# RWKV head pairs: all TensorE work in an order held by the source, with projections fed in stated numbers between the products

## The chip, the cores and the metric

The kernel runs on one core of a Trainium2 chip. The metric is the device time of one execution in microseconds (us). The kernel before takes 2841.09 us, the median of 3 runs (2839.93 to 2842.29). One more execution was taken by the hardware profiler; it took 2842.14 us, and its span, from the first to the last instruction that the profile shows, is 2839.8 us.

Five engines work side by side, each through its own queue of instructions: TensorE (PE: matrix products and transposes; PEld is its weight load), VectorE (DVE), ScalarE (ACT), GpSimd (POOL) and SyncE (SP, which here only issues transfers). They wait for each other by semaphores.

## The reference

One layer of a hybrid decoder block for x of 512 tokens by 2048 channels, in float32. One large input product gives the channels of both mixers and of two gates; the RWKV-7 mixer and a sliding-window attention run in parallel, are merged by sigmoid gates and projected out, and a gated convolutional FFN follows. The part that the change touches is the RWKV mixer with 16 heads of 64 channels:

```python
def rwkv7_mix(zs, w0, w2, a0, a2, g2, k_k, k_a, r_k, gn_w, gn_b):
    ...
    r, k, v, wd, ad, gd = jnp.split(zs, [o1, o2, o3, o4, o5], axis=-1)
    w = -jax.nn.softplus(-(w0 + jnp.tanh(wd) @ w2)) - 0.5
    decay = jnp.exp(-jnp.exp(w.astype(f32)))
    a = jax.nn.sigmoid(a0 + ad @ a2)
    g = jax.nn.sigmoid(gd) @ g2
    kk = (k * k_k).reshape(hd).astype(f32)
    kk = kk / jnp.maximum(jnp.sqrt(jnp.sum(kk * kk, axis=-1, keepdims=True)), 1e-12)
    k = k * (1.0 + (a - 1.0) * k_a)
    ...
    def step(state, inp):
        r_t, k_t, v_t, w_t, ka_t, kb_t = inp
        sa = jnp.einsum('bhvk,bhk->bhv', state, ka_t)
        state = (state * w_t[:, :, None, :] + sa[..., None] * kb_t[:, :, None, :]
                 + v_t[..., None] * k_t[:, :, None, :])
        y = jnp.einsum('bhvk,bhk->bhv', state, r_t)
        return state, y
    ...
    y = ((y - mu) * lax.rsqrt(var + GN_EPS)).reshape(B, S, RW_DIM)
    y = y * gn_w.astype(f32) + gn_b.astype(f32)
    bonus = jnp.sum(rh * kh * r_k.astype(f32), axis=-1, keepdims=True) * vh
    out = (y + bonus.reshape(B, S, RW_DIM)) * g.astype(f32)
    return out.astype(zs.dtype)
```

zs is the input product with a token shift: each channel is mixed with the token before by a factor mu of its own.

## The kernel before

The program goes through its stages in this order: norm and attention (up to about 310 us), the RWKV head pairs (332 to 1109 us), the gates that are left and the branch products (from 1109 us), the output product, and the FFN up and down.

**A projection.** Every 128 columns of the input product are a tile `acc` (128 x 512) in PSUM. It takes 48 products of TensorE: for each of 16 blocks of 128 input channels three products, since operands are split into a high and a low part (`whi`, `wlo`, `xhi`, `xlo`; L255, L256, L257). The weights come in pieces of four blocks: SP loads `raw` (L235), ScalarE rounds the high part `whi` (L238), VectorE subtracts for `wlo` (L239). Four pairs of `whi` and `wlo` are held, so 4 x 12 = 48 products can be ready ahead. In this document "projections" are these single products.

**A head pair.** The 16 heads are worked through in 8 pairs, and the recurrence in 8 chunks of 64 tokens (NCH = 8, C = 64). `early(p)` makes a pair's operands: the tiles k, r and v with the token shift (ScalarE writes `zpad`, L536, and VectorE combines, L537: `kz`, `rz`, `vz`), the norm of kk (sums of squares on TensorE, L369; eleven small steps of an inverse root on VectorE, L183 to L192; then `head_rows`, which turns the result, `rsT`, and sends it through DRAM, `rsd`, to be read back spread over the partitions, `rsb`), the decay (a lora product, tanh, a running sum `Ei` by two scans, L659, two exponentials), and `BKK`, `BAR`, the keys and queries of all chunks. `late(p)` does the pair's products: "grams" of the keys with the queries (L719, masked by VectorE into `OW` and `AM`, L722), the values transposed and centred (`VV`, L752), the decayed keys (`BKK` times `ee`, L742) transposed (L758) and copied by ScalarE (`KD`, `KO`, L762 and L763), the products for all chunks (`KV`, `GV`, L625), and then a triangular inverse built in levels m = 2, 4, 8, 16, 32. A level has a product with `AI` and one with `BT` (both L773 and L774, 16 small products each); VectorE works in between (reduce L776, mask L790, cast L791, subtract L792, into `XIW`), and behind it a transposition (L802) whose result VectorE and ScalarE copy into `BT` (L806, L808). Then comes a chain over the 8 chunks of 22 links, each a small product of TensorE that waits for VectorE or ScalarE: `psG`, `psU`, `psS`, with `G`, `UU` and the state `SS`. `final(p)` does the outputs (46 small products), the group norm (`yd`), four transposes (L855), and the gate from a lora product (L620).

**What sets the order.** Instructions of an engine run in the order in which the program holds them. A scheduler makes that order when the program is built, from the source order and its own estimates of durations; only what is wrapped in `pin` keeps the source's order. Before the change, pinned were the grams, the pair's products over all chunks (L625) and the chain's `psU`. The loop calls `late(p)`, then `early(p+1)`, `final(p)` and three gate projections (`emit_gate`), and the scheduler mixes the projections of the next pair between the products of this one. PSUM holds three `acc`, three `bulk` and two `chn` tiles.

## Time and profile before

| | us |
|---|---|
| median of 3 runs | 2841.09 |
| profiled execution | 2842.14 |
| its span | 2839.8 |
| TensorE busy in the span | 2772.6 (98%) |
| VectorE busy | 1975.7 (70%) |
| ScalarE busy | 1289.0 (45%) |
| a steady head pair (first gram to first gram, 630.51 to 729.29) | 98.78 |
| the last pair (1026.08 to the last output product, 1108.78) | 82.70 |

Times are counted from the span's start. A row of the timeline gives the start, the duration, the engine and line, the operation with what it writes and reads, and in brackets how long the engine had been idle and what ended that. A large product's duration (0.39 us) is longer than the distance to the next one's start (0.227 us), because products overlap in the array; so distances of starts are used to measure a gap. A row of the waits names the engine and line that waited, what ended the wait, the sum in us, the number of times and the longest.

### The profile page before, as it was taken

How to read it: one execution, taken by the hardware profiler on the slowest of the kernel's cores; microseconds unless marked ns; L12 is line 12 of the kernel's file. 1: busy time of each engine (PE TensorE's matmuls, PEld its weight loads, DVE VectorE, ACT ScalarE, POOL GpSimd, SP SyncE). 2: the span in 40 equal slices, each digit the busy share in tenths (PEclk: the TensorE clock that was granted, in tenths of full speed). 3: DMA queues.
4: the chain of work that ended last, by engine and by line, in shares of the span. 5: the costliest groups of instructions: out<-in, count | busy, mean ns of one | idle time of the engine just before them, and what ended most of it. 6: DMA issues, size and time to landing. Idle time of an engine off the chain costs nothing.

```text
span 2839.8 us, 48133 instructions
## 1 busy us (share of the span) xinstructions
PE 2772.6 (98%) x18722; PEld 2413.2 (85%) x18722; DVE 1975.7 (70%) x3312; ACT 1289.0 (45%) x2075; POOL 230.8 (8%) x307
## 2 busy tenths in 40 slices
PE   7999999999999999999999999999999999999999
PEld 6888777777777777788888999999999999788887
DVE  5566677778777774455668777777777778655555
ACT  5345344334433433322465555555555555444444
POOL 0101000000000001011000101010101110000000
PEclk9999999999999999999999999999999999999999
DMA  6865676676667668888777789888988897877775
GB/s 190 232 155 152 174 181 166 159 179 162 164 152 177 164 173 240 241 245 275 245 260 200 220 237 245 225 226 232 244 229 224 231 241 227 313 242 241 257 257 189
DMA packets 223860, 608.06 MB, mean 214 GB/s; under 512 B 24576, under 2 KB 44688, under 8 KB 222608
## 3 DMA queue, kind: packets, MB, share of 16 engines
q1 hardware_dynamic: 156096, 432.49, 47.4%
q0 software_dynamic: 36832, 134.24, 24.6%
q10 hardware_dynamic: 30704, 38.27, 3.9%
q8 instruction: 146, 2.39, 0.3%
q14 instruction: 82, 0.67, 0.1%
HBM read 554.23 MB, written 174.40 MB: 257 GB/s over the span
## 4 chain that ended last, share of the span: by engine, by line
PE 86%; DVE 8%; DMA 2%; issue 1%; ACT 1%; ACTq 0%; SPq 0%; DVEq 0%
PE X L1164 18%; PE X L1031 11%; PE acc L255 9%; PE acc L257 9%; PE acc L256 9%; PE Y L1031 9%; PE Y L1164 8%; PE Z L1164 4%; PE bulk L625 1%; PE bulk L773 1%; DMA raw<-in_w_z_dram 1%; PE mi L508 1%; DMA raw<-in_w_dn_dram 1%; DVE BT L741 1%; PE bulk L802 1%
## 5 line engine op out<-in xcount | busy, mean ns | idle before, releaser
L257 PE MATMUL acc<-xhi,wlo 128*128 128x512 f32 x1120 | 450.3, 402 | 6.8 <-DVE wlo L239 6.8
L255 PE MATMUL acc<-xhi,whi 128*128 128x512 f32 x1120 | 450.1, 402 | 2.4 <-ACT whi L238 2.4
L256 PE MATMUL acc<-xlo,whi 128*128 128x512 f32 x1120 | 449.1, 401 | 0.0
L238 ACT ACTIVATE whi<-raw 128x512 fp32r<-128x512 f32 x352 | 220.7, 630 | 466.7 <-PE acc L256 353.3
L1024 DVE TENSOR_TENSOR wlo<-raw,whi 128x1024 fp32r<-128x1024 f32 x210 | 257.1, 1225 | 205.9 <-ACT whi L1023 204.3
L239 DVE TENSOR_TENSOR wlo<-raw,whi 128x512 fp32r<-128x512 f32 x352 | 240.3, 688 | 183.2 <-ACT whi L238 177.3
L1023 ACT ACTIVATE whi<-raw 128x1024 fp32r<-128x1024 f32 x210 | 222.6, 1060 | 291.0 <-PE X L1031 154.2
L1164 PE MATMUL X<-b,whi 128*128 128x256 f32 x1472 | 269.2, 283 | 2.3 <-DVE u L1184 0.9
L1147 DVE TENSOR_TENSOR wlo<-raw,whi 128x1024 fp32r<-128x1024 f32 x176 | 215.1, 1223 | 76.8 <-ACT whi L1146 76.5
L1164 PE MATMUL X<-t,whi 128*128 128x256 f32 x1408 | 259.1, 284 | 8.8 <-DVE u L1184 8.3
L1164 PE MATMUL Y<-t,whi 128*128 128x256 f32 x1408 | 257.1, 283 | 0.0
L257 PEld LDWEIGHTS acc<-xhi,wlo 128*128 128x128 f32 x1120 | 211.6, 189 | 46.4 <-DVE wlo L239 10.7
L255 PEld LDWEIGHTS acc<-xhi,whi 128*128 128x128 f32 x1120 | 211.4, 189 | 40.2 <-ACT whi L238 2.8
L256 PEld LDWEIGHTS acc<-xlo,whi 128*128 128x128 f32 x1120 | 211.8, 189 | 36.0
L1146 ACT ACTIVATE whi<-a 128x1024 fp32r<-128x1024 f32 x132 | 139.4, 1056 | 214.7 <-DVE a L1140 213.3
L1164 PEld LDWEIGHTS X<-b,whi 128*128 128x128 f32 x1472 | 229.5, 192 | 3.1 <-issue 2.4
L1164 PEld LDWEIGHTS X<-t,whi 128*128 128x128 f32 x1408 | 221.0, 193 | 9.3 <-DVE u L1184 5.7
L1164 PEld LDWEIGHTS Y<-t,whi 128*128 128x128 f32 x1408 | 219.6, 192 | 0.0
L1164 PE MATMUL X<-b,wlo 128*128 128x256 f32 x736 | 208.4, 283 | 2.1 <-DVE wlo L1147 2.1
L1147 DVE TENSOR_TENSOR wlo<-a,whi 128x1024 fp32r<-128x1024 f32 x132 | 161.7, 1226 | 67.4 <-ACT whi L1146 66.7
L1164 PE MATMUL X<-t,wlo 128*128 128x256 f32 x704 | 200.1, 284 | 0.0
L1164 PE MATMUL Y<-t,wlo 128*128 128x256 f32 x704 | 199.2, 283 | 0.0
(680 smaller groups left out, 5870.3 us busy)
## 6 DMA issues: line engine op xcount, KB each, us to landing
raw<-in_w_up_dram SPq DMA_DIRECT2D x180, 512.0 KB
raw<-in_w_z_dram SPq DMA_DIRECT2D x288, 256.0 KB
s_dn<-in_w_dn_dram POOLq DMA_DIRECT2D x88, 512.0 KB, 6.5
raw<-in_w_up_dram POOLq DMA_DIRECT2D x88, 512.0 KB, 8.3
raw<-s_dn SPq DMA_DIRECT2D x88, 512.0 KB
raw<-in_w_dn_dram SPq DMA_DIRECT2D x66, 512.0 KB
a<-in_w_up_dram SPq DMA_DIRECT2D x48, 512.0 KB
s_dn<-in_w_dn_dram SPq DMA_DIRECT2D x44, 512.0 KB
```

The lines of the kernel that those rows point to most:

```text
L238: pin(act.activation(hi, raw, AF.Copy))
L239: pin(dve.tensor_tensor(lo, raw, hi.bitcast(F32), op=ALU.subtract))
L255: pe.matmul(acc, whi[:, j], xhi[:, k], start=first, stop=False)
L256: pe.matmul(acc, whi[:, j], xlo[:, k], start=False, stop=False)
L257: pe.matmul(acc, wlo[:, j], xhi[:, k], start=False, stop=last)
L508: pe.matmul(ps[:, h], pT[:, kb, h], vt[:, n - 1 + kb, g * HD : (g + 1) * HD], start=kb == kbs[0], stop=kb == kbs[-1])
L1023: act.activation(whi, wr, AF.Copy)
L1024: dve.tensor_tensor(wlo, wr, whi.bitcast(F32), op=ALU.subtract)
L1031: pe.matmul(dst, l[:, q, ts], r[:, es], start=fst and j == 0, stop=lst and j == 2, skip_group_check=True)
L1146: pin(act.activation(hi, t, AF.Copy))
L1147: pin(dve.tensor_tensor(lo, t, hi.bitcast(F32), op=ALU.subtract))
L1164: pin(pe.matmul(ps, l[:, k], r[:, k], start=start and k + i == 0, stop=last and i == 2, skip_group_check=True))
```

## The change

The pair's work is cut into methods of two classes: `Early` (the next pair's operands) and `Pair` (the products). Every product and transpose of TensorE in this stage goes through `mm` or `turn`, which pin it. Projections are made by generators, `tile_job`, one product a step; `feed(n)` issues the next n of them from a list `jobs_bg`, in the order gate, k, r, v, gate, gate for each pair, and six gates in the last pair. The source states the numbers: 38 projections, the first gram, (the previous pair's `back`: transposes of yd), 10, the second gram, 16, the transposes of OW, 18, (the previous pair's `gated`: its lora product), 24, and then in each level the AI product, 14, the BT product, 9, the transposition. Inside the levels stand now: `values` behind BT at m=2, `keys` behind BT at m=4, the next pair's sums of squares at m=8, `inputs` (KV, GV) at m=16, and behind the transposition of m=16 the next pair's `rows` and `decay`; then `rate`, 10, the chain with 3 projections behind each of 22 links, and the outputs. In all 288 projections a pair, 6 tiles. In the level's second half ScalarE's and VectorE's `XIW` now come in the source ahead of `BX`. What VectorE, ScalarE, SP and GpSimd do is still ordered by the scheduler, save that the decay of BKK is issued behind the masks of BT (`issue_after`). The number of instructions is the same on each engine.

How the built order changes is shown at three places, without the rows' numbers.

VectorE at level m=8, before (`half` is what the reduce writes, `rz` the next pair's shifted r; the reduce L776 in the sixth row answers the AI product of the level):

```order
L776 TENSOR_REDUCE half__4848<-bulk 128x8x32
L795 TENSOR_SCALAR BX<-half__4848 64x8x8x4
L798 SCALAR_TENSOR_TENSOR XIW<-half__4848,XIW 128x64x4
L537 SCALAR_TENSOR_TENSOR rz<-acc,omu,zpad_2832 128x512
L806 COPY BT<-bulk 64x8x64
L776 TENSOR_REDUCE half__4884<-bulk 128x8x32
L239 TENSOR_TENSOR wlo<-raw,whi 128x512
L806 COPY BT<-bulk 64x8x64
L790 TENSOR_TENSOR half__4884<-half__4884,cst 128x8x32
L791 CAST XIW<-half__4884 128x8x32
L239 TENSOR_TENSOR wlo<-raw,whi 128x512
L792 TENSOR_TENSOR XIW<-half__4884,XIW 128x8x32
```

and after the change (L855 is the reduce, L893 the copy into BT):

```order
L855 TENSOR_REDUCE half__5030<-bulk 128x8x32
L882 TENSOR_SCALAR BX<-half__5030 64x8x8x4
L239 TENSOR_TENSOR wlo<-raw,whi 128x512
L880 SCALAR_TENSOR_TENSOR XIW<-half__5030,XIW 128x64x4
L893 COPY BT<-bulk 64x8x64
L537 SCALAR_TENSOR_TENSOR rz<-acc,omu,zpad_2832 128x512
L855 TENSOR_REDUCE half__5104<-bulk 128x8x32
L893 COPY BT<-bulk 64x8x64
L871 TENSOR_TENSOR half__5104<-half__5104,cst 128x8x32
L239 TENSOR_TENSOR wlo<-raw,whi 128x512
L872 CAST XIW<-half__5104 128x8x32
L873 TENSOR_TENSOR XIW<-half__5104,XIW 128x8x32
```

The shift of r still stands ahead of the level's reduce, now behind one copy into BT.

ScalarE at the same place, before, where the copies into KD and KO stood ahead of the levels:

```order
L794 ACTIVATE BX<-half__8147 64x8x16x2
L797 ACTIVATE XIW<-half__8147 128x128x2
L808 ACTIVATE BT<-bulk 64x8x64 x2
L238 ACTIVATE whi<-raw 128x512
L794 ACTIVATE BX<-half__8205 64x8x8x4
L797 ACTIVATE XIW<-half__8205 128x64x4
L536 ACTIVATE zpad_2832<-acc,par 128x512
L238 ACTIVATE whi<-raw 128x512
L808 ACTIVATE BT<-bulk 64x8x64 x2
```

and after, where they stand behind the BT product of m=4 (L839 and L840):

```order
L839 ACTIVATE KD<-bulk 64x4x64
L840 ACTIVATE KO<-bulk 64x256
L879 ACTIVATE XIW<-half__8387 128x64x4
L881 ACTIVATE BX<-half__8387 64x8x8x4
L839 ACTIVATE KD<-bulk 64x4x64
L840 ACTIVATE KO<-bulk 64x256
```

Behind these rows come two more pairs of KD and KO, `zpad_2832` and the two copies into BT (L895). So eight copies into KD and KO now stand in front of r's `zpad` and of the copies into BT, with the level's `XIW` and `BX` between them.

VectorE at level m=32 and at the chain's start, after the change. Before, the level's rows from the reduce to the subtraction held only a copy into BT and two `wlo`, and `lw`, the scans, `kk` and what follows stood among the links of the chain:

```order
L855 TENSOR_REDUCE half__5380<-bulk 128x8x32
L893 COPY BT<-bulk 64x8x64
L717 TENSOR_SCALAR lw<-lw 128x512
L871 TENSOR_TENSOR half__5380<-half__5380,cst 128x8x32
L720 SCALAR_TENSOR_TENSOR Ei<-going,lw 128x256 x2
L872 CAST XIW<-half__5380 128x8x32
L239 TENSOR_TENSOR wlo<-raw,whi 128x512
L873 TENSOR_TENSOR XIW<-half__5380,XIW 128x8x32
```

```order
L202 TENSOR_TENSOR wllo<-wl,wlhi 128x256
L731 TENSOR_SCALAR k_5434<-lw,half 128x512
L709 TENSOR_TENSOR kk<-kk,rsb 128x512
L732 TENSOR_TENSOR k_5434<-k_5434,kz 128x512
L733 TENSOR_SCALAR lw<-lw 128x512
L239 TENSOR_TENSOR wlo<-raw,whi 128x512
L735 TENSOR_TENSOR kz<-kk,lw 128x512
L921 TENSOR_TENSOR SS<-KV,link 128x64
```

`lw` and the scans of `Ei` (L717, L720) have moved between the mask (L871, and ahead of it) and the cast (L872), and `kk<-kk,rsb` with three multiplies and a `wlo` ahead of the chain's first `SS`.

The diff, cut to its core ("..." marks what is left out; the methods that are not shown hold the same operations as the functions before):

```diff
+            def mm(*args, **kw):
+                pin(pe.matmul(*args, **kw))
+
+            def turn(*args):
+                pin(pe.transpose(*args))
+
+            jobs_bg = []
+
+            def tile_job(c0, done):
+                acc = accp.tile([P, S], F32, name="acc", tag="acc")
+                src = zt[c0]
+                for k0 in range(0, NK, 4):
+                    whi, wlo = load_w(src[:, k0 : k0 + 4])
+                    for j in range(4):
+                        k = k0 + j
+                        for i, (l, r) in enumerate(((whi, xhi), (whi, xlo), (wlo, xhi))):
+                            mm(acc, l[:, j], r[:, k], start=k + i == 0, stop=k == NK - 1 and i == 2)
+                            if k == NK - 1 and i == 2:
+                                done(acc)
+                            yield
+
+            def gate_job():
+                i = gates.pop(0)
+
+                def done(acc):
+                    g = gp.tile([P, S], F32, name="gt", tag="gt")
+                    act.activation(g, acc, AF.Tanh, scale=0.5)
+                    act.dma_start(gate_d[i * P : (i + 1) * P], g)
+
+                return tile_job(d.c_zr + i * P, done)
+
+            def feed(n):
+                while n and jobs_bg:
+                    if next(jobs_bg[0], True):
+                        jobs_bg.pop(0)
+                    else:
+                        n -= 1
+
...
-            def early(p):
-                wl = lp.tile([P, 2 + NG, P], F32, name="wl", tag="wl", bufs=2)
-                sync.dma_start(wl, a["lora"][p].rearrange("p (k c) -> p k c", c=P))
-                w2a2 = lora_parts(wl, 0)
...
-            def late(p, st):
-                wl, Ei, kk, kb, k2, rz, vz, bon = st
...
-                dve.tensor_tensor(BKK, BKK, ee.unsqueeze(2).to_broadcast([P, NCH, P]), op=ALU.mult)
-                ps = bulk()
-                for t in range(NT):
-                    ts = slice(t * P, (t + 1) * P)
-                    pe.transpose(ps[:, ts], vz[:, ts], ident)
-                vm = wk.tile([P, NCH], F32, name="vm", tag="vm")
...
-            def final(p, st):
-                wl, bon = st
-                ps = bulk()
-                for n in reversed(range(NCH)):
...
-            st = early(0)
...
+            class Early:
+
+                def __init__(self, p):
+                    self.p = p
+                    self.wl = lp.tile([P, 2 + NG, P], F32, name="wl", tag="wl", bufs=2)
+                    sync.dma_start(self.wl, a["lora"][p].rearrange("p (k c) -> p k c", c=P))
+
+                def jobs(self):
+                    p = self.p
+                    return [tile_job(d.c_k + p * P, self.k_in), tile_job(d.c_r + p * P, self.r_in),
+                            tile_job(d.c_v + p * P, self.v_in)]
+
...
+                def rows(self):
+                    rb = head_rows(wk, bulk(), self.rs, "lg", turn=turn)
+                    dve.tensor_tensor(self.kk, self.kk, rb, op=ALU.mult)
+
+                def decay(self):
+                    self.w2a2 = lora_parts(self.wl, 0)
+                    ps = bulk()
+                    lora(ps, self.w2a2, (0,), 0)
...
+            class Pair:
+
+                def __init__(self, st):
...
+                def decayed(self):
+                    with tc.issue_after(self.masked.ins):
+                        dve.tensor_tensor(BKK, BKK, self.st.ee.unsqueeze(2).to_broadcast([P, NCH, P]), op=ALU.mult)
+
+                def keys(self):
+                    self.KO = KO = wk.tile([P, NCH, C], F32, name="KO", tag="ko")
+                    for g in range(2):
+                        ns = slice(g * HN, (g + 1) * HN)
+                        ps = bulk().rearrange("p (n c) -> p n c", c=P)
+                        for j in range(HN):
+                            turn(ps[:, j], BKK[:, g * HN + j], ident)
+                        for lo, hi in HV:
+                            act.activation(KD[lo:hi, ns, lo:hi], ps[0:C, :, lo:hi], AF.Copy)
+                            act.activation(KO[lo:hi, ns], ps[C:P, :, lo:hi], AF.Copy)
+
+                def inputs(self):
...
+                def second(self, m):
+                    xa, IW = self.rows_of(m), self.IW
+                    t = self.by_block(self.mm3(BT, lambda n: IW[:, n].rearrange("p e c -> p (e c)"), lambda n: IW[:, n, 0]), m)
+                    if m != LEVELS[-1]:
+                        act.activation(xa[:, 0], t, AF.Copy, scale=1.0 / SG)
+                        dve.scalar_tensor_tensor(xa[:, 1], t, 1.0 / SG, xa[:, 0], op0=ALU.mult, op1=ALU.subtract)
+                    act.activation(self.altered(BX[0:C, :, 0:C], m), t[0:C], AF.Copy, scale=1.0 / (SG * SG))
+                    dve.tensor_scalar(self.altered(BX[C:P, :, C:P], m), t[C:P], 1.0 / (SG * SG), None, op0=ALU.mult)
...
+            st = Early(0)
+            for job in st.jobs():
+                jobs_bg.append(job)
+            feed(NK * 3)
+            st.stats()
+            feed(NK)
+            st.rows()
+            st.decay()
+            st.rate()
+            feed(NK * 8)
+            st.bonus()
+            st.bonus_sums()
+            gone = None
             for p in range(NP):
-                lt = late(p, st)
-                if p + 1 < NP:
-                    st = early(p + 1)
-                final(p, lt)
-                for _ in range(GATES_PER_PAIR * NK // 16):
-                    emit_gate()
+                last = p == NP - 1
+                nxt = None if last else Early(p + 1)
+                own = [] if last else nxt.jobs()
+                others = [gate_job() for _ in range(min(len(gates), 6 if last else GATES_PER_PAIR))]
+                jobs_bg += others[:1] + own + others[1:]
+                do = Pair(st)
+                st.dense()
+                st.rows_r()
+                if gone:
+                    gone.scaled()
+                feed(38)
+                do.gram(0)
+                if gone:
+                    gone.back()
+                feed(10)
+                do.gram(HN)
+                do.start_x()
+                feed(16)
+                do.start_a()
+                feed(18)
+                do.start_rest()
+                if gone:
+                    gone.gated()
+                feed(24)
+                do.decayed()
+                for m in LEVELS[1:]:
+                    i = LEVELS.index(m)
+                    do.first(m)
+                    feed(14)
+                    do.second(m)
+                    if i == 1:
+                        do.values()
+                    if i == 2:
+                        do.keys()
+                    if nxt and i == 3:
+                        nxt.stats()
+                    if i == 4:
+                        do.inputs()
+                    if m != LEVELS[-1]:
+                        feed(9)
+                        do.turned()
+                    if nxt and i == 4:
+                        nxt.rows()
+                        nxt.decay()
+                if nxt:
+                    nxt.rate()
+                feed(10)
+                for i, _ in enumerate(do.chain()):
+                    feed(3)
+                    if nxt and i == 2:
+                        nxt.bonus()
+                    if nxt and i == 6:
+                        nxt.bonus_sums()
+                do.outputs()
+                gone, st = do, nxt
+            gone.scaled()
+            feed(30)
+            gone.back()
+            feed(12)
+            gone.gated()
+            feed(1000)
 
 
         xbs = ExitStack()
```

384 lines of the change are left out of this document (201 added, 183 removed).

## The prediction

> **What bounds the kernel now.** I read the page first, then the stretches of the RWKV stage one by one, then what TensorE waits for there, then single rows around the waits. From the page:
>
> ```profile
> span 2839.8 us, 48133 instructions
> PE 2772.6 (98%) x18722; PEld 2413.2 (85%) x18722; DVE 1975.7 (70%) x3312; ACT 1289.0 (45%) x2075; POOL 230.8 (8%) x307
> PEclk9999999999999999999999999999999999999999
> ```
>
> TensorE is busy for 98% of the span at the full granted clock. So only its gaps can be won or lost, and a changed order of the same products moves time only through gaps. The next view cuts the span into a steady pair, the last pair, the projections behind it, and a stretch of bare large products. Its columns are the length, the busy time of PE, PEld, DVE, ACT and POOL, the granted clock, the share of the DMA engines, and GB/s:
>
> ```profile
> 630.51:729.29 98.78, 96.05 (x757) 75.06 (x756) 74.60 (x168) 39.53 (x81) 7.09 (x9) 1.00 0.69 167
> 1026.08:1108.78 82.70, 79.95 (x683) 61.77 (x683) 58.65 (x128) 31.85 (x66) 5.68 (x7) 1.00 0.71 178
> 1108.78:1165.00 56.22, 53.86 (x236) 43.96 (x235) 18.52 (x28) 18.62 (x32) 11.47 (x17) 1.00 0.96 299
> ```
> ```profile
> 1260.00:1330.00 70.00, 70.00 (x310) 57.98 (x309) 35.05 (x57) 18.19 (x30) 7.29 (x10) 1.00 0.82 257
> ```
>
> Bare products start every 70.00/310 = 0.226 us (0.227 below). A steady pair holds about 300 of that width (288 projections, 12 lora and similar): 68.1 us. The rest, about 30.7 us, is small products and gaps. The waits that have a name, over all pairs (total, times, longest):
>
> ```profile
> PE bulk L758 <- DVE BKK L742: 7.1, 7, 1.0
> PE acc L257 <- DVE wlo L239: 6.8, 8, 0.8
> PE bulk L855 <- DVE yd L851: 3.6, 8, 0.5
> ...
> PE psG L814 <- DVE SS L828: 0.6, 1, 0.6
> ```
>
> One pair's rows show what they cost, as start to start less 0.227:
>
> ```profile
> 644.72 0.39 PE L256 MATMUL acc<-xlo,whi 128*128 128x512 f32 x1
> 646.13 1.06 PE L758 MATMUL bulk<-ident,BKK 128*128 128x128 f32 x8 [1.01 <-DVE BKK L742]
> ...
> 647.49 0.40 PE L256 MATMUL acc<-xlo,whi 128*128 128x512 f32 x1
> 648.74 0.50 PE L257 MATMUL acc<-xhi,wlo 128*128 128x512 f32 x1 [0.84 <-DVE wlo L239]
> ...
> 674.47 0.47 PE L255 MATMUL acc<-xhi,whi 128*128 128x512 f32 x1
> 674.78 0.39 PE L256 MATMUL acc<-xlo,whi 128*128 128x512 f32 x1
> ...
> 677.30 0.39 PE L255 MATMUL acc<-xhi,whi 128*128 128x512 f32 x1
> 677.81 0.19 PE L773 MATMUL bulk<-XIW,BT 128*128 128x64 f16 x1
> ```
>
> The wait for BKK is 1.18, for wlo 1.02, for yd about 0.6 (0.45 named, plus its entry). Entry into the second product of a level costs 677.81 - 677.30 - 0.227 = 0.28 here, about 1 us over five levels; transposes and grams wait some 0.5 more. Together about **4.1 us of waits in a pair**, 4% of it. The first projection behind a group of small ones takes 0.31 (674.47 to 674.78), 0.08 extra.
>
> **The change part by part.** No instruction is added or removed on any engine. What changes is TensorE's order, and with it, since the order of the vector, scalar and DMA queues is still made by the scheduler around it, what stands in front of what there.
>
> These rows of VectorE stand behind the next steps (start, duration):
>
> ```profile
> 631.05 0.69 DVE L239 TENSOR_TENSOR wlo<-raw,whi 128x512 fp32r<-128x512 f32 x1 [2.02 <-ACT whi L238]
> ...
> 642.79 1.22 DVE L741 TENSOR_TENSOR BT<-AI,cst 64x1024 f16<-64x1024 f16 x1
> ...
> 644.75 1.23 DVE L742 TENSOR_TENSOR BKK<-BKK,ee 128x1024 f32<-128x1024 f32 x1
> ...
> 647.27 0.69 DVE L748 TENSOR_REDUCE vm<-bulk 128x8 f32<-128x512 f32 x1
> 647.99 0.69 DVE L239 TENSOR_TENSOR wlo<-raw,whi 128x512 fp32r<-128x512 f32 x1
> ```
>
> *Removed.* The groups of projections fall from 42 to about 37 in a pair: 5 x 0.08 = -0.4. BKK's transposes move from straight behind the decay multiply into level m=4, over 50 projections (11 us) later: -1.2. yd's transposes now have the first gram and 38 projections ahead of them: -0.6. The wait for wlo came of a vector queue without a weight split from 631.05 to 647.99; now the longest such run is two splits of A and gn (0.69 each, like wlo), two masks and BKK, 3 x 0.69 + 2 x 1.22 + 1.23 = 5.7 us, or 25 projections, and four split buffers hold 48: -1.0.
>
> *Added.* In each level the source now fixes 14 projections between the AI product and the BT product: 0.31 + 13 x 0.227 = 3.26 us. In that time VectorE must reduce, mask, cast and subtract. From 674.47 to 677.81 that chain took 3.34 us with one BT copy and one weight split in it, so 14 projections cover it and nothing else; whatever more stands in front of the subtraction is a wait of TensorE, one for one. The scheduler of before gave 7 to 17. The rows of VectorE, of ScalarE and of SP's queue that price what more stands there:
>
> ```profile
> 592.24 0.17 DVE L192 SCALAR_TENSOR_TENSOR rq<-rq,rq 128x8 f32<-128x8 f32 x1
> 593.05 0.28 DVE L374 COPY rsT<-bulk 8x128 f32<-8x128 f32 x1 [0.65 <-PE bulk L372]
> ...
> 595.77 0.68 DVE L659 TENSOR_TENSOR_SCAN Ei<-going,lw 128x256 f32<-128x256 f32 x1
> ...
> 601.55 0.69 DVE L649 TENSOR_TENSOR kk<-kk,rsb 128x512 f32<-128x512 f32 x1 [0.40 <-DMA rsb<-rsd]
> ...
> 634.91 1.40 DVE L722 TENSOR_TENSOR OW<-bulk,cst 64x512 f32<-64x512 f32 x2 [0.40 <-PE bulk L719]
> ...
> 649.27 1.72 DVE L752 TENSOR_TENSOR VV<-bulk,vm 64x256 f32<-64x256 f32 x4
> ...
> 653.91 0.69 DVE L776 TENSOR_REDUCE half__7006<-bulk 128x256 f32<-128x512 f32 x1
> ...
> 665.85 0.75 DVE L537 SCALAR_TENSOR_TENSOR rz<-acc,omu,zpad 128x512 f32<-128x512 f32 x1 [0.29 <-ACT zpad L536]
> 666.52 0.41 DVE L806 COPY BT<-bulk 64x512 f16<-64x512 f16 x1
> 666.85 0.67 DVE L776 TENSOR_REDUCE half__7122<-bulk 128x256 f32<-128x512 f32 x1
> ```
> ```profile
> 646.79 0.38 ACT L762 ACTIVATE KD<-bulk 64x256 f32<-64x256 f32 x1 [1.01 <-PE bulk L758]
> ...
> 649.93 0.69 ACT L536 ACTIVATE zpad<-acc,par 128x512 f32<-128x512 f32 x1
> ...
> 659.86 1.21 ACT L808 ACTIVATE BT<-bulk 64x512 f16<-64x512 f16 x2 [1.47 <-DVE BT L806]
> ```
> ```profile
> 593.36 0.29 SPq L376 DMA_DIRECT2D rsd<-rsT  x1
> ...
> 597.59 1.12 SPq L380 DMA_DIRECT2D rsb<-rsd  x2
> ```
>
> By level, in the queue order of the changed program:
>
> - m=2. Before, VectorE worked without a pause from the second gram's eviction to the first reduce, 653.91 - 634.91 = 19.0. The values leave this run (VV 1.72, vm 0.85) and one split (0.6); gn and a lora split enter (1.1): 16.9, begun 0.5 after the gram, since the first gram's evictions and the previous pair's gn are just done. TensorE has 58 projections, OW's transposes, six lora products and AI in that time, 15.7, and the reduce could start 0.2 later. It is 1.5 late at most, 0.3 if splits fall out: I take **1.0**.
> - m=4. VV (1.72) and the mean of v (0.85) now stand in front of the BT copy and the reduce. VectorE comes to the copy about 0.8 late: **0.7** (0.2 to 1.1).
> - m=8. ScalarE's queue gets eight KD and KO copies of 0.38 with X and BX between them, then zpad 0.69, then BT 1.21. From the end of the BT product at m=4 (t), ScalarE waits 0.6 for four transposes, so zpad ends at t+5.2. rz on VectorE waits for it, and behind rz stand the reduce and a BT copy. The reduce could start at t+4.1 and starts at t+5.9: **1.4** (0.5 to 1.8).
> - m=16. Eleven small steps of the root (0.17 each) stand between copy, reduce and cast, half of them ahead: **0.4** (0.05 to 0.8).
> - m=32. lw (0.43) and two scans (0.68 each) stand between mask and cast, and lw waits for a tanh behind BT's 1.21: **1.3** (0.3 to 1.8).
> - Chain. kk waits for the norm's round trip through DRAM, 601.55 - 593.05 = 8.5 from rsT, and behind it in VectorE's queue stand kk, k's multiply, lw, a split and kz (4 x 0.69 as kk's row and 0.43 for lw, 3.2) and then the first SS, for which the product of G waits. From rsT TensorE has AI, 14 projections, the wait at m=32, BT, three lora products, ten projections and two links, 10.5: between 0 (DMA early) and 2; **1.2**, nearer to the row. SP's queue carries rsd and rsb as before; raw loads behind rsd wait from 593.36 to 597.59, 4.2 us, under four filled split buffers (48 projections, 10.9 us).
> - Gram and links: **0.3**.
>
> Sum 6.3 us of waits in place of 4.1, less 0.4 of returns: **+1.8 in each of seven pairs, +12.6**. The last pair has no next pair's k, r, v, norm or decay in its queues: 0.3 + 0.7 + 0.3 + 0.3 = 1.6 in place of 4.2, and the returns: **-3.0**.
>
> *Moved.* Three gates go from behind the last pair into pairs, so 168 and not 248 projections cover the loads of the branch stage: 38 us and not 56. The stall there is today:
>
> ```profile
> PE acc L255 <- ACT whi L238: 2.4, 1, 2.4
> ```
>
> It falls about 37 us after the last pair, with DMA at 0.96 in the row above, so loads are behind already. It stays, and up to 4 more may come since the branch weights are wanted 18 us sooner: **+0.5** (-2 to +4). Gate writes and the pair's output write move on ACT's and GpSimd's queues; nobody waits for them before the branch stage.
>
> Sum: 12.6 - 3.0 + 0.5 = +10.1 on the profiled execution's 2842.1 us, which is 1.05 above the median: **2851 us**.
>
> **The rivals.**
>
> *Faster: the fixed counts do cover the queues.* If VectorE and ScalarE reach each reduce on time, the five entries cost 0.28 as at 677.81 and the chain nothing: 1.4 + 0.3 + some 0.2 = 1.9 of waits, -2.2 - 0.4 in a pair, x 7 = -18, -3 for the last: 2841 - 21 = **2820**. For it: BKK, wlo and yd really go, 2.8 in a pair. Against it: at 665.85 rz waited 0.29 for zpad, and the BT copy (666.52) and reduce (666.85) behind it were issued only after it, though the copy's input does not depend on it. A late ScalarE thus delays the reduce. It decides if the lag at an entry is under 0.3.
>
> The Trainium skill, "TensorE: Matmul & The Clock Gate", in the table at its top (row "Engine queue depth"), has ScalarE and VectorE as strict first-in-first-out queues; by that rule this rival needs the queues short, and the trace agrees, with the 0.29 just named.
>
> *Same: the lags are half of mine.* 6.0/2 + 0.3 + 0.9 (entries that remain) = 4.2, returns -0.4: -0.3 x 7 - 3 + 0.5 = -4.6: **2837**. For it: VectorE has 24 us idle in a pair of 98.78 and can catch up.
>
> *Slower still: the norm's round trip or the loads of the tail decide.* If the row comes back 2 us later than 8.5, as in the one pair where G waited 0.6 even with the old order, each of seven pairs pays 1.8 more, or the branch stage pays 4: **2855 to 2868**.
>
> *The clock falls.* If the granted clock went to half for the next 7 projections after each of some 42 new stalls, each stall would lose 7 x 0.227 = 1.6 more: 2851 + 67 = **2918**. Against it: the steady pair with stalls of 1.18 and 1.02 only 2.6 us apart shows a granted clock of 1.00, and so does the stretch with a stall of 2.4.
>
> The Trainium skill, "TensorE: Matmul & The Clock Gate", section "A second HAM failure mode: psum-queue depth-cycling", says that frequent short idles between groups of products can make the clock gate swing to half rate, which is the rule behind this rival; by that rule alone the pair before should have shown it, and the trace does not agree, with its 1.00.
>
> *The change does not do what it says.* TensorE's order is pinned, so it does; but the other queues are not pinned, and my lags rest on their built order.
>
> **How the numbers follow.** A measurement of this kernel can tell 0.2%, 5.7 us, from no change: faster is below 2835.4, slower above 2846.8. My forecast (lags of 5 to 7.5 in a pair) has 0.44, slower still 0.14, the clock 0.02, same 0.22, faster 0.18. A tenth of my forecast's share lies below 2846.8, and a twentieth of the same case below 2835.4, which gives slower 0.56, same 0.25, faster 0.19. The forecast's own range is 2845 to 2859; with the other cases the range is **2827 to 2865**, which leaves out the far half of faster and the end of slower still.
>
> **What would show it.** Right: waits for BKK, yd and wlo are gone from TensorE's list; in their place stand waits of the BT product (XIW, from the subtraction) of 0.5 to 1.5 at m=2, 4, 8 and 32, and one of G for SS; steady pairs of 100 to 101 us, the last of 79 to 80. Wrong: XIW waits below 0.3 each and pairs near 96 would mean that the queues keep up (faster); a G wait over 2 us or a stall over 4 ahead of the branch stage would mean the rival on the slow side; a granted clock below 1.00 in pairs would mean the rival of the clock.

## The result, and the profile after

The changed kernel takes 2882.64 us, the median of 4 runs (2878.38 to 2883.53), against 2841.69 us (2839.93 to 2843.97) of the kernel before: a ratio of 1.0137 with a 95% interval of 1.0123 to 1.0150. It is slower by 1.4%, some 41 us, four times the 10 us that the prediction named. The profiled execution took 2878.38 us (the lowest of its four runs), its span is 2876.6 us, so 36.8 us longer than before's.

The page of the changed kernel, its head and the row of PE, DVE and ACT:

```profile
span 2876.6 us, 48139 instructions
PE 2781.3 (97%) x18722; PEld 2444.3 (85%) x18722; DVE 1972.3 (69%) x3312; ACT 1289.6 (45%) x2075; POOL 229.9 (8%) x307
```

TensorE has the same products as before and is busy for 8.7 us longer in total; the other 28 us are idle time. Busy time is itself a sum of two things, products that ran longer and short delays that went away; they are taken apart below. What TensorE waits for between 300 and 1250 us of the changed kernel (total, times, longest):

```profile
PE bulk L610 <- DVE XIW L873: 30.2, 33, 1.5
PE link L610 <- DVE SS L921: 14.0, 7, 3.2
PE acc L255 <- ACT rhi L201: 3.7, 1, 3.7
PE bulk L610 <- ACT lg L690: 3.1, 1, 3.1
PE acc L255 <- ACT whi L238: 2.4, 1, 2.4
PE bulk L613 <- DVE yd L944: 0.4, 1, 0.4
```

The waits for BKK, for wlo and (but for one) for yd are gone, as forecast. In their place stand the waits of the BT products for XIW, and one wait in each of seven pairs for SS at the chain's start. New in kind are the waits for `lg` and `rhi`, which the prediction did not have.

Stretches of the changed kernel, and the same stretches of the kernel before. From the second pair's first gram to the last pair's (six steady pairs), and from the last output product of the pairs to the first branch product:

```profile
445.42:1061.07 615.65, 577.15 (x4531) 467.88 (x4531) 445.06 (x1008) 238.70 (x481) 42.66 (x54) 0.98 0.66 159
...
1148.00:1198.58 50.58, 44.02 (x187) 35.08 (x185) 13.99 (x24) 12.19 (x22) 9.71 (x15) 0.97 0.90 272
```
```profile
432.16:1026.08 593.92, 576.78 (x4532) 450.22 (x4531) 447.20 (x1008) 237.16 (x481) 42.57 (x54) 1.00 0.67 165
...
1108.78:1167.96 59.18, 56.82 (x250) 46.40 (x248) 18.52 (x28) 18.62 (x32) 11.47 (x17) 1.00 0.91 284
```

With 4531 products in both, six pairs take 21.7 us longer, 3.6 in each, and the granted clock is 0.98 where it was 1.00. The rest of the 36.8 us by stretches, with what merely changed place (38 projections, 8.6 us, now stand ahead of the first gram; a lora and yd's transposes, 1.8 us, stand behind a gram) taken out:

| stretch | longer by, us |
|---|---|
| up to the end of attention | 1.0 |
| from there to the first gram (70.65 before, 85.65 after, less 8.6) | 6.4 |
| first pair | -0.9 |
| six steady pairs | 21.7 |
| last pair and the projections behind it | 2.4 |
| branch stage, up to the first output product | 1.9 |
| the rest, up to the end | 4.3 |

**One pair's long wait, and the clock behind it.** Rows of TensorE at the chain's start in one pair of the changed kernel:

```profile
717.59 0.40 PE L610 MATMUL acc<-xhi,wlo 128*128 128x512 f32 x1
721.20 0.69 PE L610 MATMUL link<-SS,BAR 128*128 128x64 f32 x2 [3.21 <-DVE SS L921]
721.65 0.77 PE L610 MATMUL acc<-xhi,whi 128*128 128x512 f32 x1
722.23 0.63 PE L610 MATMUL acc<-xlo,whi 128*128 128x512 f32 x1
722.65 0.63 PE L610 MATMUL acc<-xhi,wlo 128*128 128x512 f32 x1
```

Behind a wait of 3.4 us the products of 512 columns start 0.42 us apart (722.23 to 722.65) and not 0.227. The same place cut at the grid on which the clock changes:

```profile
717.62:721.04 3.42, 0.37 (x2) 0.00 (x0) 2.85 (x6) 0.63 (x1) 0.00 (x0) 1.00 0.30 106
721.04:724.45 3.41, 3.25 (x10) 2.76 (x11) 2.39 (x6) 0.23 (x1) 0.00 (x0) 0.50 0.50 92
724.45:727.86 3.41, 3.41 (x12) 2.83 (x11) 1.24 (x4) 0.00 (x0) 0.00 (x0) 0.50 0.70 218
727.86:731.28 3.42, 3.42 (x17) 2.30 (x16) 1.79 (x4) 1.76 (x4) 0.81 (x1) 1.00 0.27 19
```

The granted clock is 0.50 for two stretches of 3.41 us. Over the whole execution such stretches lose 37.7 us of clock in the changed kernel and 9.5 us in the kernel before (half their length, summed over the records). Not all of it costs time, since TensorE stands idle in part of them. Counting for each product that starts in such a stretch what it took over the median of its kind, at most double, gives 6.4 us before and 30.6 us after: by this estimate the clock costs about 24 us more. The waits that the profile names grew as well, from 22.6 to 54.0 us between 300 and 1250 us. The two together are more than 36.8, so some 18 us came back elsewhere. In the six steady pairs the parts are 21.4 us more of idle time, about 12 us of clock, and about 12 us that came back: TensorE's busy time is 577 us in both kernels although some products of the changed one ran at half clock, mostly because it now enters the transposes and the links with shorter delays.

The pairs show the price of the clock by themselves. The one steady pair without a half-clock stretch takes 99.3 us, the two with one stretch take 101.9 and 102.3, and the three with two take 103.8, 103.8 and 104.6. Less what they wait longer for SS and at the levels, that is 1.5 to 1.6 us for each of eight stretches.

What VectorE did at that place, and what it waited for:

```profile
707.16 0.27 DVE L374 COPY rsT<-bulk 8x128 f32<-8x128 f32 x1
...
718.18 0.69 DVE L709 TENSOR_TENSOR kk<-kk,rsb 128x512 f32<-128x512 f32 x1 [2.93 <-DMA rsb<-rsd]
...
720.93 0.21 DVE L921 TENSOR_TENSOR SS<-KV,link 128x64 f32<-128x64 f32 x1
```

The round trip through DRAM took 11.0 us here and not 8.5, VectorE stood 2.9 us at kk, and SS came 2.7 us behind kk, as its place in the queue said. Over the six steady pairs kk started 8.9 to 11.0 us behind rsT, 10.1 in the mean; in the eight pairs of the kernel before it was 8.0 to 9.5. The wait of TensorE follows this time: 1.3 us at 8.9, 3.4 at 11.0. Why the round trip became longer is not shown.

### The profile page after: what moved, and what is told of

Read it like the earlier page. It is cut to its first block, busy times and chain, and to the rows that moved or that the text cites. A ratio compares the mean times of both kernels' runs of the same rounds, so it can differ in the third digit from the quotient of the medians.

```text
span 2876.6 us, 48139 instructions
## 1 busy us (share of the span) xinstructions
PE 2781.3 (97%) x18722; PEld 2444.3 (85%) x18722; DVE 1972.3 (69%) x3312; ACT 1289.6 (45%) x2075; POOL 229.9 (8%) x307
## 4 chain that ended last, share of the span: by engine, by line
PE 85%; DVE 6%; DMA 3%; ACT 3%; issue 2%; ACTq 0%; SPq 0%; DVEq 0%
PE X L1329 17%; PE acc L610 16%; PE X L1196 10%; PE Y L1196 9%; PE Y L1329 8%; PE acc L255 4%; PE acc L256 4%; PE acc L257 4%; PE Z L1329 4%; PE bulk L610 3%; PE bulk L663 1%; PE link L610 1%; PE bulk L613 1%; DMA raw<-in_w_z_dram 1%; DVE wlo L239 1%
## 5 line engine op out<-in xcount | busy, mean ns | idle before, releaser
L1188 ACT ACTIVATE whi<-raw 128x1024 fp32r<-128x1024 f32 x210 | 222.6, 1060 | 289.5 <-PE X L1196 148.3
L610 PE MATMUL acc<-xhi,whi 128*128 128x512 f32 x816 | 344.8, 423 | 0.0
L610 PE MATMUL acc<-xlo,whi 128*128 128x512 f32 x816 | 327.4, 401 | 0.0
L610 PE MATMUL acc<-xhi,wlo 128*128 128x512 f32 x816 | 326.6, 400 | 0.0
L1311 ACT ACTIVATE whi<-raw 128x1024 fp32r<-128x1024 f32 x176 | 184.4, 1049 | 20.7 <-ACT whi L1311 14.7
L1196 PE MATMUL X<-whi,hhi 128*128 128x512 f32 x480 | 187.6, 391 | 0.7 <-ACT u L1345 0.7
L1196 PE MATMUL X<-whi,hlo 128*128 128x512 f32 x480 | 188.1, 392 | 0.0
```

Of the source, the lines that this page charges most:

```text
L610: pin(pe.matmul(*args, **kw))
L1188: act.activation(whi, wr, AF.Copy)
L1196: pe.matmul(dst, l[:, q, ts], r[:, es], start=fst and j == 0, stop=lst and j == 2, skip_group_check=True)
L1311: pin(act.activation(hi, t, AF.Copy))
```

## The experiments

Ratios are to the kernel before, measured on the same chip beside each; the changed kernel's own is 1.0137. The waits by level are start-to-start distances of TensorE less 0.227, means over six steady pairs; in the changed kernel they are 0.46, 1.20, 1.65, 0.31 and 1.28 us at m=2, 4, 8, 16, 32, and 2.5 (1.3 to 3.4) for SS.

**The norm one level earlier.**

```diff
-                    if nxt and i == 3:
+                    if nxt and i == 2:
                         nxt.stats()
...
-                    if nxt and i == 4:
+                    if nxt and i == 3:
                         nxt.rows()
+                    if nxt and i == 4:
                         nxt.decay()
```

> Edit: the next pair's sums of squares stand one level earlier (m=4) and its norm's round trip through DRAM one level earlier (m=8); all else as in the changed kernel. Theory (two mechanisms: the wait for SS behind the round trip, mean 2.4 us in a steady pair, and the granted clock that falls after it, about 2 us in a steady pair): the wait for SS falls below 0.3, the granted clock in the pairs is 1.00 again, a steady pair takes 98.5 to 99.5 us, about -4 x 7 = -28 us, 2850 to 2858. Rival (the clock falls because of the short BT waits, not of the long one): the wait for SS goes but the clock still falls to 0.97 to 0.98 in the pairs, a steady pair takes about 101, -15 us, 2866 to 2872.

Measured: 2858.66 us, ratio 1.0045 (1.0030 to 1.0060). SS no longer waits, but neither number came in whole: a steady pair takes 100.0 us in the mean, and BT at m=32 now waits 2.3 to 3.7 where it had waited 1.3. The wait moved, and the clock still falls once at that place in five of the six pairs. What VectorE waits for in the steady pairs of this kernel:

```profile
DVE kk L709 <- DMA rsb<-rsd: 17.9, 6, 3.6
```

It stands at kk for 3.0 us in each pair. The scheduler put this multiply into level m=16, ahead of the copies and the reduce of m=32, and VectorE does not go past it.

**The same, with the multiply used late.** The multiply of kk by the norm's row is issued behind that of k2:

```diff
-                    rb = head_rows(wk, bulk(), self.rs, "lg", turn=turn)
-                    dve.tensor_tensor(self.kk, self.kk, rb, op=ALU.mult)
+                    self.rb = head_rows(wk, bulk(), self.rs, "lg", turn=turn)
...
-                    dve.tensor_tensor(k2, k2, self.kz, op=ALU.mult)
+                    after = dve.tensor_tensor(k2, k2, self.kz, op=ALU.mult)
...
+                    with tc.issue_after(after.ins):
+                        dve.tensor_tensor(self.kk, self.kk, self.rb, op=ALU.mult)
```

> Edit: as the kernel with the earlier norm alone, but the multiply of kk by the norm's row, which waits for the round trip through DRAM, is issued on VectorE behind the multiply of k2, at the chain's start, in place of at m=16. Theory (in that kernel the waits of 2.3 to 3.7 us at BT of m=32 were VectorE standing at this multiply, with the copies and the reduce of m=32 behind it): BT at m=32 is back at 1.3 in every pair, SS waits 0.3 to 1.0 since the multiply's 0.69 is ahead of it but waits for nothing; a steady pair takes 97.5 to 99, the clock stays at 1.00 in nearly all pairs, 2842 to 2850 against 2858.7. Rival (VectorE is simply overfull between m=16 and the chain): the time lost moves to SS, 2855 to 2862.

Measured: 2841.37 us, ratio 0.9995 (0.9986 to 1.0005). BT at m=32 waits 1.31 in every pair, SS 0.48, a steady pair takes 97.6 us where the clock stays up (four of six) and 98.8 where it fell once. The run before differs in the place of this one multiply, and was slower by 0.0050 of the time, some 14 us: that is the price of an operation that waits for a transfer at the head of VectorE's queue, with the clock that follows. Against the changed kernel the two edits of the norm together are worth some 40 us (1.0137 to 0.9995), as much as the change lost. Not all of that is the round trip: in a pair SS waits 2.0 us less and the levels m=8 and m=16 together 1.2 less, the half-clock stretches in steady pairs fall from eight to two, and up to 4 us may be the part behind the pairs, of which more below. The other waits of the levels are still there, 3.7 us in a pair, near the 4.1 that the prediction counted in the kernel before.

**More projections in the levels.**

```diff
-                feed(38)
+                feed(23)
...
-                    feed(14)
+                    feed((16, 20, 22, 17, 21)[i - 1])
...
-                    feed(3)
+                    feed(3 - i % 2)
```

> Edit: between the AI and the BT product of the levels m=2, 4, 8, 16, 32 stand 16, 20, 22, 17, 21 projections in place of 14 each; the 26 come from the 38 ahead of the first gram (now 23) and from the chain (3 and 2 by turns in place of 3). Theory (14 projections are too short for the vector queue, and what is late is late by 0.5, 1.2, 1.65, 0.3, 1.27): the BT waits fall from 4.9 us in a steady pair to under 1, nothing of it comes back elsewhere but some tenths in the chain; the wait for SS shrinks by about 1.5 since the round trip has one level of 21 instead of 14 to run in; clock losses shrink with it: -5 to -7 us in a pair, 2830 to 2845. Rival (VectorE is the bound of the whole stretch, so a wait taken away at one level returns at the next or in the chain): waits keep their sum, time 2875 to 2885.

Measured: 2838.53 us, ratio 0.9980 (0.9971 to 0.9989), in the theory's range. BT waits fall from 4.9 to 0.7 in a pair, no half clock in the pairs. Something comes back: SS and the chain's first product wait for VectorE, which stands at kk, and links wait for it where two projections cover them:

```profile
PE link L610 <- DVE SS L921: 7.8, 13, 1.0
PE link L610 <- DVE BX L882: 7.2, 6, 2.2
```

**Both together** (the earlier norm and the larger numbers).

> Edit: the earlier norm and the larger numbers in the levels together. Theory: waits of a steady pair under 2 us in all, clock 1.00, a steady pair 93 to 95.5 us, about -8 us x 7 and -1.5 in the last pair, 2815 to 2832, faster than the kernel before by 0.3% to 0.9%. Rival (VectorE is the bound): not better than the earlier norm alone, 2850 or more.

Measured: 2827.44 us, ratio 0.9940 (0.9925 to 0.9954). Five of six steady pairs are 94.6 to 95.6 us, the clock falls in none. VectorE was not the bound; the order and the counts were.

**The start.** On top of both, the first sums of squares stand behind 64 projections:

```diff
-            feed(NK * 3)
+            feed(NK * 4)
             st.stats()
```

> Edit: as the kernel with the earlier norm and the larger numbers in the levels, and at the stage's start the first sums of squares stand behind 64 projections and not behind 48. Theory (they stood straight behind the last product of k's tile, and waited 3.3 us for shift, k_k and square, and the clock fell behind that): the wait of 3.3 and the half clock of 6.8 us (3.4 lost) at the start go, -5 to -7 us, 2820 to 2823. Rival (the wait is a late weight load or VectorE's queue and moves to the next place): -2 us or less, 2825 to 2828.

Measured: 2821.31 us, ratio 0.9919 (0.9903 to 0.9935), 6 us less. The two intervals overlap, so the times alone do not show the step; the profiles do, where the stretch from the end of attention to the first gram takes 75.7 us in place of 80.6. In the changed kernel TensorE waited here for the square of kk, and then ran at half clock:

```profile
307.82 0.39 PE L610 MATMUL acc<-xhi,wlo 128*128 128x512 f32 x1
311.32 1.79 PE L610 MATMUL bulk<-cst,lg 128*128 128x2 f32 x8 [3.11 <-ACT lg L690]
...
313.54 0.63 PE L610 MATMUL acc<-xlo,whi 128*128 128x512 f32 x1
313.96 0.63 PE L610 MATMUL acc<-xhi,wlo 128*128 128x512 f32 x1
```

The 48th projection ends k's tile, and the sums that need its shift, its scaling and its square came straight behind it.

**The keys back ahead of the levels.**

```diff
                 do.decayed()
+                do.keys()
...
-                    if i == 2:
-                        do.keys()
```

> Edit: the changed kernel with the transposes of the decayed keys and their copies by ScalarE back ahead of the levels, straight behind the decay, as in the kernel before. Theory (at m=8 eight copies stand ahead of zpad on ScalarE, and rz, ahead of the reduce on VectorE, waits for it): the BT wait at m=8 falls from 1.65 to 0.3 to 0.9, a wait for BKK of 1 to 1.6 comes back, BT at m=2 falls below 0.4: within 5 us of the changed kernel, 2876 to 2884. Rival (VectorE's own work at m=8 is the cause, not ScalarE's copies): BT at m=8 stays above 1.3, and with the wait for BKK the time is 2888 to 2895.

Measured: 2875.97 us, ratio 1.0118 (1.0103 to 1.0133), the lower edge of the theory's range, by other terms than it said. BT at m=8 fell from 1.65 to 0.2, below the range, and rz no longer waits for zpad, so the eight copies ahead of zpad were its cause. These rows of the changed kernel, of ScalarE and of VectorE, had shown it:

```profile
793.12 0.38 ACT L840 ACTIVATE KO<-bulk 64x256 f32<-64x256 f32 x1
793.53 0.69 ACT L536 ACTIVATE zpad<-acc,par 128x512 f32<-128x512 f32 x1
```
```profile
794.25 0.75 DVE L537 SCALAR_TENSOR_TENSOR rz<-acc,omu,zpad 128x512 f32<-128x512 f32 x1 [1.09 <-ACT zpad L536]
794.92 0.68 DVE L855 TENSOR_REDUCE half__8461<-bulk 128x256 f32<-128x512 f32 x1
```

No wait for BKK came back. BT at m=2 fell to 0 in place of it, BT at m=4 rose from 1.20 to 1.86, and the transposition behind m=2 waited 0.7 for the X that ScalarE now makes behind the copies. The sum of the levels is smaller by 0.5 us in a pair; SS waited 3.2 and not 2.5.

**The wait filled with narrow products.**

```diff
+                            if n == 1:
+                                for _ in range(14):
+                                    mm(ps, BX[:, 0], GV[:, 0], start=True, stop=True)
```

> Edit: 14 additional small products (0.14 us each, into a tile that the next product overwrites; the output is the same) stand in front of the chain's first G product, where TensorE waits for SS: the wait is filled with work instead of taken away. Theory (the clock falls since TensorE stands idle): the filled wait keeps the clock at 1.00 in most pairs, the time until SS comes stays, a steady pair takes about 2 us less, total -8 to -14 us, 2868 to 2875. Rival (the clock loss has nothing to do with that idle time): the clock in the pairs stays 0.97 to 0.98 and the time is the same or up to 5 us longer, 2881 to 2888.

Measured: 2887.99 us, ratio 1.0147 (1.0130 to 1.0164): the rival's time, but not for its reason. The scheduler gave VectorE another order here (a wlo and BKK ahead of G), G waits for it 1.2 us more, and behind the fill SS is still late; the clock fell in five of six steady pairs, three times at the chain's start and four times around m=8. It does not tell the two apart.

**The wait filled with wide products.**

```diff
+                            if n == 1 and self.nxt:
+                                pw = bulk()
+                                for _ in range(16):
+                                    mm(pw, self.nxt.w2a2[0][:, 0], lhi[:, 0], start=True, stop=True)
```

> Edit: as the kernel with the filled wait, but the filling is 16 products of 512 columns (0.227 us each, 3.6 us in all, into a PSUM tile that nobody reads) in place of 14 products of 64 columns. Theory (the clock of a fixed stretch of 3.41 us falls when the stretch before had fewer than about 2600 columns streamed into TensorE): no fall of the clock behind the chain's start any more in any pair, those behind the BT product of m=8 stay in up to four pairs, clock loss in the pairs 2 to 7 us in all in place of about 13; the wait for G that the scheduler's order makes (1.2) stays; time 2874 to 2886 (the filling itself can cost 0.5 us in a pair). Rival (the clock falls by idle time alone, or by the levels' small products): falls behind the chain's start in three or more pairs, 2886 to 2894.

Measured: 2887.83 us, ratio 1.0165 (1.0138 to 1.0191). Behind the chain's start the clock falls in one pair, the one where SS and G still waited 2.7 us together, and around m=8 in four. The count of falls is close to the theory's, the time is the rival's: 16 products cost 3.7 us in a pair and replace a wait of 2.5 in the mean, and G waits 0.8 to 1.8 in four pairs. How a fall comes about at m=8, with a wait of only 1.5 us, is in these stretches of this kernel:

```profile
692.87:696.28 3.41, 1.94 (x27) 1.82 (x27) 2.38 (x7) 0.00 (x1) 0.00 (x0) 1.00 0.44 84
696.28:699.69 3.41, 3.41 (x12) 2.40 (x11) 1.97 (x9) 1.25 (x3) 0.47 (x1) 0.50 0.67 198
```

In the first TensorE was busy for 1.94 us with 27 products, but nearly all are narrow (2 to 64 columns); the next runs at half clock.

**A version that beats both.** As with both and the start, 22 projections at m=4 and 21 ahead of the first gram:

```diff
-                feed(23)
+                feed(21)
...
-                    feed((16, 20, 22, 17, 21)[i - 1])
+                    feed((16, 22, 22, 17, 21)[i - 1])
```

> Edit: earlier norm, later first sums of squares, and the numbers in the levels 16, 22, 22, 17, 21 with 21 projections ahead of the first gram. Theory: the BT wait at m=4 (0.6 to 0.9 in five pairs with 20) goes, nothing new ahead of the gram: 0.5 us in a pair below the kernel with 20, 2816 to 2820. Rival: yd or the gram waits for VectorE behind only 21 projections, and the time is 2820 to 2826.

Measured: 2819.47 us, ratio 0.9915 (0.9900 to 0.9930). BT at m=4 no longer waits but in one pair. In time this is not told apart from the run with both and the start (0.9919). The first three pairs still lose 1.3 to 2.1 us in the transposition at m=16, for the reason known by then (VectorE of this kernel):

```profile
587.53 0.69 DVE L709 TENSOR_TENSOR kk<-kk,rsb 128x512 f32<-128x512 f32 x1 [3.65 <-DMA rsb<-rsd]
588.14 0.42 DVE L880 SCALAR_TENSOR_TENSOR XIW<-half__6405,XIW 128x256 f16<-128x256 f32 x1
```

**The same, with the multiply late.** It is issued behind the decay's scans:

```diff
-                        dve.tensor_tensor_scan(Ei[:, hs], going, lg[:, hs], 0.0, op0=ALU.mult, op1=ALU.add)
+                        after = dve.tensor_tensor_scan(Ei[:, hs], going, lg[:, hs], 0.0, op0=ALU.mult, op1=ALU.add)
+                    with tc.issue_after(after.ins):
+                        dve.tensor_tensor(self.kk, self.kk, self.rb, op=ALU.mult)
```

> Edit: as the kernel with 22 projections at m=4, with the multiply of kk by the norm's row issued on VectorE behind the decay's scans at m=32. Theory (in that kernel the transposition at m=16 waited 1.3 to 2.1 us in the first three pairs for the low part of X, which stood on VectorE behind this multiply): these three waits go, BT at m=32 gets at most 0.4 in each pair: -2 to -5 us, 2815 to 2818. Rival (the slow round trip is met later in the same pairs, at m=32): the same time within 1.5 us.

Measured: 2815.94 us, ratio 0.9908 (0.9891 to 0.9924), 26 us below the kernel before. The three waits are gone, BT at m=32 waits 0.38 in each pair, and every steady pair takes 94.9 to 95.1:

```profile
523.27:618.21 94.94, 94.18 (x757) 75.47 (x756) 74.13 (x169) 39.56 (x80) 7.07 (x9) 1.00 0.68 172
```

Its interval overlaps that of the version before it, so the step itself is not shown in the time, only in the waits.

## Why the prediction was wrong

The side was right, the size was not: 2851 us forecast with a range up to 2865, 2882.6 measured. By the prediction's own steps:

- **What goes.** BKK, yd and wlo were to give back 2.8 us in a pair, and did. The returns of 0.4 for fewer groups came too (37 groups in a pair where there were 43), but they were only a part: about 2 us in a pair came back as busy time in all, as said above.
- **The lags of the levels** were forecast at 1.0, 0.7, 1.4, 0.4, 1.3, in sum 4.8, and measured at 0.46, 1.20, 1.65, 0.31, 1.28, in sum 4.9. The reading of the queues by rows held; m=2 was too high, m=4 too low. That the eight copies make m=8 late was tested and is so.
- **The chain** was the first term that failed. It was taken at 1.2 us between 0 and 2, and measured at 1.3 to 3.4, 2.5 in the mean: +1.3 in a pair. The queue behind the transfer was read rightly; the transfer itself was mis-sized, priced by one pair of before (8.5 us) where the changed kernel took 10.1 in the mean; at 8.5 the wait would have been some 0.9, by the steady pairs' own wait less their round trip. The rival "slower still" had this mechanism, a row that comes 2 us later, and gave it 0.14; by its own price the time would have been 2855 to 2868, so it was a part of the miss and not the whole.
- **The clock** was the step that failed most. The rival had 0.02, on the ground that the steady pair before, with stalls of 1.18 and 1.02, and the stretch with a stall of 2.4, showed 1.00. Both readings are right, but neither bears out what was drawn from them. In that pair the poorest stretch of the grid still held four large products and eight transposes, 3072 columns in all. The stall of 2.4 in the kernel before happened to be cut in two by the grid:

```profile
1143.88:1147.29 3.41, 2.26 (x10) 1.52 (x9) 0.00 (x0) 0.00 (x0) 0.81 (x1) 1.00 1.05 298
1147.29:1150.70 3.41, 2.20 (x8) 1.53 (x9) 1.52 (x3) 2.12 (x4) 0.00 (x0) 1.00 1.07 338
```

  so that 8 and 9 large products start in its two stretches. The falls behind a wait of SS had 0 to 3 in theirs. So a wait that empties a stretch costs up to 1.7 us more, half of the next one. The section that the prediction named beside this rival and set aside, the Trainium skill, "TensorE: Matmul & The Clock Gate", section "A second HAM failure mode: psum-queue depth-cycling", has short idles between groups of products make the clock swing; the 0.50 in the rows above agrees. In steady pairs this cost about 2 us each, 12 us in six, where the forecast had none. The rival's own 2918 (a fall behind each of 42 stalls) was too much: seven falls in the pairs, one of two stretches. Two of the prediction's own signs of being wrong came: a wait for SS over 2 us in five of six pairs, and a granted clock of 0.97 to 0.98 in the same five.
- **The start** had no term. The prediction counted the products ahead of the first gram and did not ask what `feed(NK * 3)` puts straight behind the last product of k's tile: 3.3 us of wait and a fall of the clock, 6.4 in all; the run that moved the sums by 16 projections took some 6 off.
- **The last pair and the tail** were to give -2.5 us together and took 2.4 more. The last pair's waits at BT are 1.6, near the forecast. The stall at the raw loads stayed at 2.4, also as forecast; behind it comes a wait of 3.7 for `rhi`, ahead of the branch stage, with the clock at half twice. The prediction held that nobody waits for the gate writes ahead of the branch stage, and that step failed. ScalarE's rows there:

```profile
1186.54 0.63 ACT L238 ACTIVATE whi<-raw 128x512 fp32r<-128x512 f32 x1 [6.30 <-DMA raw<-in_w_z_dram]
...
1189.54 0.33 ACTq L364 DMA_DIRECT2D gate_d<-gt  x1
1196.88 0.60 ACT L363 ACTIVATE gt<-acc 128x512 f32<-128x512 f32 x1 [7.37 <-DMA gate_d<-gt]
1197.37 0.62 ACT L201 ACTIVATE ahi<-ain 128x512 fp32r<-128x512 f32 x1
```

  The tile `gt` has one buffer. The last gate's tanh therefore stood until the write of the gate before it had landed, 7.3 us after its issue, and `ahi` and `rhi` stood behind it. That gate in turn was late behind a `whi` that waited for its load. The loads that are short of cover had been given up to 4 us, but at the middle of the range 0.5.
- **After the pairs** the same program lost 4.3 us more from the first output product to the end. Its waits are the same there; the clock was lower (0.97 against 0.99 in the stretch of some 258 us behind that product). Up to TensorE's last product that part takes 1492.8 to 1497.2 us in the twelve profiles, with no relation to the edits: 1492.8 to 1494.4 where two or three stretches of it run at half clock, 1496.3 to 1497.2 where five do, as in the changed kernel. So the likeliest reason is where the waits of that part fall on the grid of the clock; no run was made for that alone.

Two sets of experiments show how the terms hang together. With the norm earlier and its multiply late, the time is 2841.4, no slower than before: so what is left of the forecast's terms, with the start and the tail that it left out, sums to about no change. The rival "the fixed counts do cover the queues" at 2820 was not what this change did, but is what the same pinned order does with other counts: 2816 to 2821.

## What to carry to other kernels

When projections are put between dependent products by fixed numbers, each number must cover the longest of the other engines' queues at that place, not the bare chain: count what stands in front, above all an operation that waits for a transfer, because everything behind it in its queue is late with it. A product must not be placed straight behind the last one that makes its input. Price a wait of TensorE with what it does to the clock: several short waits, or one wait beside narrow products, can cost as much again.

## What the runs showed of the hardware

The granted clock changes on a fixed grid of 3.41 us: in every one of the twelve profiles all half-clock stretches begin at multiples of it from each other, whatever the kernel did. Summing, from the profiles' rows, the columns of the products that start in a stretch (behind 330 us, clock at full), 62 of 63 stretches with fewer than 2560 columns (a third of the 7700 that back-to-back products stream) were followed by half clock, and of some 8640 with 2560 or more only 14 were, all at 2560 to 3072. That is a correlation over twelve kernels; the fills meant to prove it by intervention were only in part conclusive. The Trainium skill, "TensorE: Matmul & The Clock Gate", section "HAM oscillation — how this bites in real kernels", gives the rule as no idle gap over about 3.4 us; here idle gaps of 1.5 us beside narrow products were enough, and one of 2.4 us among wide ones, cut in two by the grid, was not. TensorE in the changed kernel, behind the wait at m=8 of one pair:

```profile
796.03 0.39 PE L610 MATMUL acc<-xhi,whi 128*128 128x512 f32 x1
797.92 0.59 PE L610 MATMUL bulk<-XIW,BT 128*128 128x64 f16 x16 [1.50 <-DVE XIW L873]
798.36 1.03 PE L610 MATMUL bulk<-cst,lg 128*128 128x2 f32 x8
...
799.58 0.63 PE L610 MATMUL acc<-xhi,wlo 128*128 128x512 f32 x1
800.01 0.63 PE L610 MATMUL acc<-xhi,whi 128*128 128x512 f32 x1
```

The large products from 799.58 on start 0.43 apart.
